# A decoder block on one core: two products of a Strassen-Winograd pair change places, the next pair's weight splits follow them, and the last combinations go between chunks of p4

## The chip, the core and the metric

The kernel runs on one core of one Trainium2 chip. Its time is the device time of one execution in microseconds; the times shown for the kernel before come from three runs. The profile is one further execution, recorded by the hardware profiler; its own time is given beside its span, because the two differ a little. The engines are named as the profile names them: PE (matmuls, with PEld for weight loads), DVE (vector), ACT (scalar), POOL (GpSimd) and SP (which here only issues transfers).

## What is computed

The reference is one decoder layer on 512 tokens of width 1024 in float32:

```python
h = rmsnorm(x, pre_mix_norm)
proj = h @ w_in          # q_r, k_r, v_r, g_r, q_s, k_s, v_s, gate_r, gate_s
ret = silu(g_r) * groupnorm(retention(q_r, k_r, v_r))
y_r = ret @ w_ret_out
y_s = swa_gqa_sinks(q_s, k_s, v_s, sinks) @ w_swa_out
merged = sigmoid(gate_r) * y_r + sigmoid(gate_s) * y_s
x = x + rmsnorm(merged @ w_out, post_mix_norm)
h = rmsnorm(x, pre_mlp_norm)
u = square(relu(h @ w_up))            # 1024 -> 4096
x = x + rmsnorm(u @ w_down, post_mlp_norm)   # 4096 -> 1024
```

## The kernel before, in words

**Precision by splitting.** Every large product is made of three matmuls in a reduced format: an operand is split into a high part and a low part (`split`, L119 to L122). ACT casts the high part (L121), DVE subtracts it from the source to get the low part (L122). `mm3` (L162 to L166) then multiplies high by high (L164), high by low (L165) and low by high (L166). In the profile a line of `split` or `mm3` stands for all of its callers, so groups are told apart by the names of the tiles: `whi` and `wlo` are split weights from the pool `stream`, `p` (in the code p24 and p22) are split weights from the pool `wx` or `px`.

**Gate and up projections in pairs.** The two gate projections (8 pairs of 256 columns: r and s in turn) and 13 of the 16 pairs of the up projection use a seven-product scheme for 2x2 blocks (Strassen-Winograd). For one pair, `wino_weights` (L203) prepares the left operands from two tiles: `raw`, which `wino_load` (L196) fills by two SP transfers (L199, L200: a11 and a12 in one, a22 in the other), and `rs`, the sums s1 and s3, which `wino_sums` (L189) fills by one SP transfer (L192) and one accumulating POOL transfer (L193). It splits a11 and a12 (p1: `whi`, `wlo`), then rs (p31: `whi`, `wlo`), adds a11 and a12 into rs (L208, L209), splits that into p24 (s2 and s4) and splits a22 into p22. `wino_pair` (L221) then issues the products in the order 11·11, 12·21, s2·t2, s4·22, s1·t1, s3·t3, 22·t4. Each `product` is four `mm3`, that is 12 matmuls, so a pair is 84 matmuls. Around them DVE and ACT combine the banks: L240 to L242 after the first three products, L246 and L249 after s1·t1 and s3·t3, L251 last.

**What limits how far ahead the weights are made.** `raw` has two buffers, `whi` and `wlo` four each, `rs` two in the gate stage and three in the up stage, p24 and p22 one each. So p24 of the next pair can be written only when s4·22 of this pair is done, and p22 only when 22·t4 is done. The transfer into a `raw` buffer waits until the pair that used the buffer has made its last split from it, which is p22's. In the profile p22's parts appear as `p<-raw` and p24's as `p<-rs`.

**Who sets the order.** Each engine executes its queue in order. The queues are laid out when the kernel is built, from the order of the source lines as priority and from when operands and buffers come free; so a line that stands earlier in the source goes first when both are ready, but the queues are not simply the source order. `tc.high_priority` moves a block ahead.

**Callers.** In the gate stage `gate` (L698) makes the weights of a pair, runs `wino_pair`, applies the sigmoid on ACT (L711) and for s multiplies into ys (L713). After the pairs r and s of each of the first three `bp` comes `ret_proj` (L717), which loads 1024 KB of w_ret_out into a `raw` buffer (L137), splits it into two `whi`/`wlo` pairs and makes two blocks of 24 matmuls (tile `yr`). In the up stage `up_pair` (L922) does the same for w_up with relu and square on ACT (L933, L934), into the tile `uc`.

**The end of the kernel.** The down projection is another seven-product scheme over 4 chunks `j` of the inner dimension, with two token blocks `tb`. p1, p2 and p5 come first, then p6, p3 and p7 interleaved (L1071 to L1079). L1082 to L1090 combine p6, p3 and p7 on DVE and call `finish` (L1018), which squares and sums on ACT (L1023), scales on DVE (L1027, L1028 or L1031, L1035, L1038), takes a power on POOL (L1034) and stores (L1041). Then p4 is made: chunks 0 and 1 (24 matmuls each), then chunks 2 and 3 for each token block in turn (24 matmuls each), with the last combination L1101 and `finish` after each block. For each chunk `left` (L954) splits the activations and `right` (L959) the summed weights `tch` in two halves; `left` has two buffers.

Of the kernel before, what the change touches and what calls it, by code (L numbers as in the profile page):

```python
# [20 lines left out]
KD = D_MODEL // P  # L21
# [70 lines left out]
def block_kernel(ctx, tc, x, pre_mix, w_in, w_gate, w_ret, w_swa, w_out, sinks, post_mix,  # L92
                 pre_mlp, w_up, w_down, post_mlp, decay, chunk, dist, out):
    nc = tc.nc
    x, out = x[0], out[0]
# [100 lines left out]
    def wino_load(w):  # L196

        raw = raw_tile([P, 3, 4, P])
        nc.sync.dma_start(raw[:, 0:2], w[:, 2:4])  # L199
        nc.sync.dma_start(raw[:, 2], w[:, 0])  # L200
        return raw

    def wino_weights(wx, rs, raw, px=None):  # L203

        a11, a12, a22 = raw[:, 0], raw[:, 1], raw[:, 2]
        p1 = parts(raw[:, :2], [P, 2, 4, P])
        p31 = parts(rs, [P, 2, 4, P])
        nc.vector.tensor_tensor(rs[:, 0], rs[:, 0], a11, op=ALU.add)  # L208
        nc.vector.tensor_tensor(rs[:, 1], rs[:, 0], a12, op=ALU.add)  # L209
        p24 = [(px or wx).tile([P, 2, 4, P], F32R, name=f"p24{i}") for i in range(2)]  # L210
        split(p24[0], p24[1], rs)
        p22 = [wx.tile([P, 4, P], F32R, name=f"p22{i}") for i in range(2)]
        split(p22[0], p22[1], a22)
        return {
            "11": tuple(a[:, 0] for a in p1), "12": tuple(a[:, 1] for a in p1),
            "22": tuple(p22),
            "s1": tuple(a[:, 0] for a in p31), "s3": tuple(a[:, 1] for a in p31),
            "s2": tuple(a[:, 0] for a in p24), "s4": tuple(a[:, 1] for a in p24),
        }

    def wino_pair(wx, a, b, out):  # L221

        p16 = bank([P, 2, 256], "wino")
        p57 = bank([P, 2, 256], "wino")
        p2 = bank([P, 256], "wino")
        p34 = bank([P, 2, 256], "wino")

        def product(ps, x, y):
            for k in range(4):
                mm3(  # L230
                    ps, tuple(o[:, k] for o in a[x]), tuple(o[:, k] for o in b[y]),
                    k == 0, k == 3,
                )

        pc = wx.tile([P, 256], F32, name="pc", bufs=2)
        q = wx.tile([P, 3, 256], F32, name="q")
        product(p16[:, 0], "11", "11")
        product(p2, "12", "21")
        product(p16[:, 1], "s2", "t2")
        nc.scalar.copy(pc, p16[:, 0])  # L240
        nc.vector.tensor_tensor(out[:, 0], p2, pc, op=ALU.add)
        nc.vector.tensor_tensor(q[:, 0], pc, p16[:, 1], op=ALU.subtract)  # L242
        product(p34[:, 0], "s4", "22")
        product(p57[:, 0], "s1", "t1")
        product(p57[:, 1], "s3", "t3")
        nc.vector.tensor_tensor(  # L246
            q[:, 1:3], p57, q[:, 0:1].to_broadcast([P, 2, 256]), op=ALU.add
        )
        nc.vector.tensor_tensor(out[:, 3], p57[:, 0], q[:, 2], op=ALU.add)  # L249
        product(p34[:, 1], "22", "t4")  # L250
        nc.vector.tensor_tensor(out[:, 1:3], p34, q[:, 1:3], op=ALU.add)  # L251


    hctx = ExitStack()
# [350 lines left out]
    for h in range(RET_HEADS):  # L605
# [20 lines left out]
        g = load_feature_pair(w_in, C_GR + h * RET_DV)  # L626
# [47 lines left out]
    wx = wino_pool(gctx)  # L674
# [20 lines left out]

    rsum = [gate_sums(0)]

    def gate(name, bp):  # L698
        i = bp + (KD // 2 if name == "s" else 0)
        if len(rsum) < len(gates):  # L700
            rsum.append(gate_sums(len(rsum)))
        a = wino_weights(wx, rsum[gates.index((name, bp))], wino_load(w_gate[i]))
        if name == "s":
            g = sgpool.tile([P, 4, 256], F32, name="sgs", bufs=1)
        else:
            g = sgpool.tile([P, 4, 256], F32, name="sgr", bufs=4)
        wino_pair(wx, a, hB, g)
        for b in range(2):
            fb = 2 * bp + b
            sg = g[:, 2 * b : 2 * b + 2].rearrange("p h c -> p (h c)")  # L710
            nc.scalar.activation(sg, sg, AF.Sigmoid, scale=(1.0, -1.0)[b])  # L711
            if name == "s":
                nc.vector.tensor_tensor(ys[fb], ys[fb], sg, op=ALU.mult)  # L713
            else:
                sig[fb] = sg

    def ret_proj(bp):  # L717

        wr = load_feature_pair(w_ret, bp * 256)
        for b in range(2):  # L720
# [7 lines left out]
            nc.vector.tensor_tensor(sig[fb], ps, sig[fb], op=ALU.mult)  # L728
            nc.vector.tensor_add(sig[fb], sig[fb], ys[fb])

    for bp in range(KD // 2):
        gate("r", bp)
        gate("s", bp)
        if bp in YR_AT:
            ret_proj(YR_AT[bp])
    gctx.close()
# [178 lines left out]
    def load_t(j):  # L915
        pool = dpool2 if j == 0 else dpool3
        tch[j] = pool.tile([P, 4, 512], F32, name=f"tch{j}")
        nc.sync.dma_start(tch[j], w_down[0, 0, j])

    usum = []  # L920

    def up_pair(fp):  # L922
        while len(usum) < 16 - NH and len(usum) < fp - NH + 3:
            f = len(usum) + NH
            pool, bufs = (dpool2, 1) if f % 3 == 2 else (rspool, 2)
            usum.append(wino_sums(pool, w_up[f], bufs))
        a = wino_weights(wx, usum[fp - NH], wino_load(w_up[fp]), px)
        j, i = fp // 4, fp % 4
        r = uc[j][:, :, i]
        wino_pair(wx, a, h2B, r)  # L930
        for b in range(2):
            rb = r[:, 2 * b : 2 * b + 2]
            nc.scalar.activation(rb, rb, AF.Relu, scale=(1.0, -1.0)[b])  # L933
            nc.scalar.activation(rb, rb, AF.Square)  # L934
        if i == 3:
            nc.vector.tensor_tensor(uc[j][:, 1], uc[j][:, 3], uc[j][:, 1], op=ALU.subtract)

    load_t(0)
    for fp in range(NH, 16):
        up_pair(fp)  # L940
    uctx.close()
    dpool3 = ctx.enter_context(tc.tile_pool(name="dpool3", bufs=1))
    for j in range(1, 4):
# [7 lines left out]
    def banks2(name):  # L951
        return [bank([P, 512], name) for _ in range(2)]

    def left(j, q):  # L954
        hi, lo = (ring.tile([P, 4, 256], F32R, name=f"left{i}") for i in range(2))
        split(hi, lo, uc[j][:, q])
        return hi, lo

    def right(src):  # L959
        return [parts(src[:, 2 * i : 2 * i + 2], [P, 2, 512]) for i in range(2)]  # L960
# [8 lines left out]
    def product2(ps, j, a, b):  # L969
        for h in range(2):  # L970
            for tb in range(2):
                product(ps, a, b, h, j == 0, j == 3, tb)
# [106 lines left out]
    step_p7(3)  # L1079


    for tb in range(2):  # L1082
        nc.vector.tensor_tensor(p15[tb], p6[tb], p15[tb], op=ALU.subtract)
        nc.vector.tensor_tensor(u3[tb], p6[tb], p1c[tb], op=ALU.subtract)
        nc.vector.tensor_tensor(p1c[tb], p3[tb], p15[tb], op=ALU.add)
        finish(tb, 1, p1c[tb])
        nc.vector.tensor_tensor(u3[tb], p7[tb], u3[tb], op=ALU.add)
        v = fin.tile([P, 512], F32, name="c", bufs=4)
        nc.vector.tensor_tensor(v, p7[tb], p15[tb], op=ALU.add)
        finish(2 + tb, 1, v)  # L1090


    p4 = banks2("p4")
    for j in range(2):
        product2(p4, j, left(j, 3), right(tch[j]))
    ab = [(left(j, 3), right(tch[j])) for j in (2, 3)]
    for tb in range(2):
        for j in (2, 3):
# [33 lines left out]
```

## Time and profile before

| what | value |
|---|---|
| median of 3 runs (lowest, highest) | 770.73 us (764.59, 771.12) |
| the profiled execution's own time | 767.67 us |
| its span, first to last instruction | 765.9 us |
| PE busy | 746.0 us, 4676 matmuls |
| DVE busy | 538.1 us |
| ACT busy | 392.5 us |
| gate stage with the retention projections between | about 255 to 390 us of the span |
| pairs of the up stage | about 462 to 600 us |
| down projection and end | about 600 to 766 us |

How to read it: the profiled execution took 767.67 us, of which 1.77 us lie outside the span. A busy PE is not PE at its peak, since the ends of matmuls are modelled; what can be read off is where PE waited and for whom. A row of the waits gives "engine line waited for: us in total, times, longest us". A row of a timeline gives the start, the duration, the engine, the line, and in brackets the idle time before it and who ended it. A row of the table by stretches gives for each engine the busy time and in parentheses the number of instructions, then the granted TensorE clock (1.00 is full), the share of the DMA engines and GB/s.

### The profile page before, as it was taken

What the parts mean: (1) busy time and instruction counts of PE and PEld (TensorE: products, weight loads), DVE (VectorE), ACT (ScalarE), POOL (GpSimd) and SP (SyncE); (2) the same over time, 40 slices, a digit from 0 to 9 for tenths busy, and PEclk for the clock granted to TensorE, in tenths of its full rate; (3) what the DMA queues carried; (4) which work ended last, traced back from release to release, by engine and by line L of the source; (5) the groups of instructions that cost most, each with busy time, mean ns of one, the idle gap of its engine ahead of it and who ended that gap; (6) DMA issues with size and microseconds to landing.
All of it is one profiled execution on the core that took longest, in us unless ns stands there. A gap on an engine that the chain in (4) does not pass through costs nothing.

```text
span 765.9 us, 11626 instructions
## 1 busy us (share of the span) xinstructions
PE 746.0 (97%) x4676; PEld 670.0 (87%) x4676; DVE 538.1 (70%) x823; ACT 392.5 (51%) x627; POOL 49.7 (6%) x65
## 2 busy tenths in 40 slices
PE   7999999999999999999999999999999999999986
PEld 6989889898888989899888999999989888888864
DVE  5473484564868966766754876867678688988795
ACT  6354463464454634343543764545466565655551
POOL 1100000000001000000001100000000010010000
PEclk9999999999999999999999999999999999999998
DMA  8151312302016566452572517765563899199511
GB/s 287 36 150 45 110 56 84 110 28 83 29 56 151 150 202 173 124 143 79 203 294 79 152 43 224 203 157 153 174 165 97 277 304 216 56 185 200 110 55 55
DMA packets 50007, 105.22 MB, mean 137 GB/s; under 512 B 2977, under 2 KB 30753, under 8 KB 46114
## 3 DMA queue, kind: packets, MB, share of 16 engines
q1 hardware_dynamic: 44914, 78.80, 30.6%
q0 software_dynamic: 5040, 25.69, 18.1%
q8 instruction: 36, 0.59, 0.3%
q14 instruction: 17, 0.14, 0.1%
HBM read 102.38 MB, written 2.10 MB: 136 GB/s over the span
## 4 chain that ended last, share of the span: by engine, by line
PE 72%; DMA 11%; DVE 9%; issue 4%; ACT 3%; POOL 0%; SPq 0%; POOLq 0%; DVEq 0%; ACTq 0%
DMA raw<-in_w_up 6%; PE pblk L166 5%; PE wino L166 5%; PE pblk L165 5%; PE pblk L164 5%; PE wino L164 5%; PE wino L165 5%; PE p L165 4%; PE p L166 4%; PE p L164 4%; DVE wlo L122 2%; PE ptok L166 2%; PE ptok L164 2%; PE ptok L165 2%; PE yr L165 2%
## 5 line engine op out<-in xcount | busy, mean ns | idle before, releaser
L122 DVE TENSOR_TENSOR wlo<-raw,whi 128x1024 fp32r<-128x1024 f32 x91 | 110.8, 1221 | 98.3 <-ACT whi L121 90.9
L121 ACT CAST whi<-raw 128x1024 fp32r<-128x1024 f32 x91 | 95.1, 1050 | 116.3 <-PE pblk L165 36.5
L165 PE MATMUL p<-wlo,left 128*128 128x512 f32 x224 | 87.5, 391 | 2.4 <-DVE wlo L122 2.3
L166 PE MATMUL p<-whi,left 128*128 128x512 f32 x224 | 87.5, 391 | 1.2 <-DVE left L122 1.0
L164 PE MATMUL p<-whi,left 128*128 128x512 f32 x224 | 87.1, 390 | 0.1
L166 PE MATMUL pblk<-hT,wlo 128*128 128x512 f32 x160 | 62.4, 390 | 0.5 <-DVE wlo L122 0.5
L164 PE MATMUL pblk<-hT,whi 128*128 128x512 f32 x160 | 62.6, 391 | 0.0
L165 PE MATMUL pblk<-hT,whi 128*128 128x512 f32 x160 | 62.3, 390 | 0.0
L165 PEld LDWEIGHTS p<-wlo,left 128*128 128x128 f32 x224 | 42.0, 188 | 12.1 <-DVE wlo L122 3.2
L166 PEld LDWEIGHTS p<-whi,left 128*128 128x128 f32 x224 | 42.0, 188 | 11.3 <-DVE left L122 2.8
L164 PEld LDWEIGHTS p<-whi,left 128*128 128x128 f32 x224 | 42.0, 188 | 9.4 <-ACT left L121 0.9
L164 PE MATMUL ptok<-whi,hT 128*128 128x256 f32 x160 | 46.5, 290 | 0.6 <-ACT hT L121 0.6
L166 PE MATMUL ptok<-whi,hT 128*128 128x256 f32 x160 | 45.9, 287 | 1.1 <-DVE hT L122 1.1
L165 PE MATMUL ptok<-wlo,hT 128*128 128x256 f32 x160 | 45.8, 286 | 0.0
L121 ACT CAST left<-uc 128x1024 fp32r<-128x1024 f32 x28 | 29.3, 1050 | 28.1 <-PE p L165 28.1
L122 DVE TENSOR_TENSOR wlo<-tch,whi 128x1024 fp32r<-128x1024 f32 x32 | 38.6, 1219 | 5.2 <-ACT whi L121 5.2
L121 ACT CAST whi<-tch 128x1024 fp32r<-128x1024 f32 x32 | 33.4, 1047 | 12.9 <-PE p L166 8.1
L122 DVE TENSOR_TENSOR left<-uc,left 128x1024 fp32r<-128x1024 f32 x28 | 34.1, 1220 | 7.9 <-ACT left L121 7.9
L166 PEld LDWEIGHTS pblk<-hT,wlo 128*128 128x128 f32 x160 | 30.0, 188 | 7.2 <-DVE wlo L122 0.9
L164 PEld LDWEIGHTS pblk<-hT,whi 128*128 128x128 f32 x160 | 30.1, 188 | 5.8
L165 PEld LDWEIGHTS pblk<-hT,whi 128*128 128x128 f32 x160 | 30.0, 188 | 5.8
L166 PE MATMUL wino<-h2s,p 128*128 128x256 f32 x104 | 30.2, 291 | 4.4 <-DVE p L122 4.1
(291 smaller groups left out, 2196.1 us busy)
## 6 DMA issues: line engine op xcount, KB each, us to landing
tch<-in_w_down POOLq DMA_DIRECT2D x10, 1024.0 KB, 10.1
raw<-in_w_in SPq DMA_DIRECT2D x9, 1024.0 KB, 5.5
raw<-in_w_down SPq DMA_DIRECT2D x7, 1024.0 KB, 8.5
rs<-in_w_up SPq DMA_DIRECT2D x13, 512.0 KB, 4.6
rs<-in_w_up POOLq DMA_DIRECT2D x13, 512.0 KB, 5.6
raw<-in_w_up SPq DMA_DIRECT2D x13, 512.0 KB, 5.3
raw<-in_w_in SPq DMA_DIRECT2D x12, 512.0 KB, 4.2
raw<-in_w_gate SPq DMA_DIRECT2D x8, 512.0 KB, 5.8
```

The costliest lines, as they stand in the source:

```text
L121: nc.scalar.copy(hi, src)
L122: nc.vector.tensor_tensor(lo, src, f(hi), op=ALU.subtract)
L164: nc.tensor.matmul(ps, ah, bh, start=first, stop=False)
L165: nc.tensor.matmul(ps, ah, bl, start=False, stop=False)
L166: nc.tensor.matmul(ps, al, bh, start=False, stop=last)
```

## The change

Three edits. In `wino_pair` the product 22·t4 moves from the last place to the fifth, straight behind s4·22, and a callback `then` is called there: it makes the weights of the next pair, so that their loads and splits stand in the source behind the last use of s2, s4 and a22 and ahead of s1·t1, s3·t3 and what combines them. The gate and up stages are rewritten around that: the weights of the first pair are made before the loop, and each pair returns the next pair's. In the gate stage the weights of the next r pair so come ahead of `ret_proj`, which stood ahead of them. At the end, the combinations of p6, p3 and p7 become a function `combine(tb)`, called behind chunk 0 of p4 for token block 0 and behind chunk 1 for block 1. No operation is added or removed.

```diff
-    def wino_pair(wx, a, b, out):
+    def wino_pair(wx, a, b, out, then=None):
...
         product(p34[:, 0], "s4", "22")
+        product(p34[:, 1], "22", "t4")
+        nxt = then() if then else None
         product(p57[:, 0], "s1", "t1")
         product(p57[:, 1], "s3", "t3")
         nc.vector.tensor_tensor(
             q[:, 1:3], p57, q[:, 0:1].to_broadcast([P, 2, 256]), op=ALU.add
         )
         nc.vector.tensor_tensor(out[:, 3], p57[:, 0], q[:, 2], op=ALU.add)
-        product(p34[:, 1], "22", "t4")
         nc.vector.tensor_tensor(out[:, 1:3], p34, q[:, 1:3], op=ALU.add)
+        return nxt
...
-    def gate(name, bp):
-        i = bp + (KD // 2 if name == "s" else 0)
+    def gate_weights(n):
+        name, bp = gates[n]
         if len(rsum) < len(gates):
             rsum.append(gate_sums(len(rsum)))
-        a = wino_weights(wx, rsum[gates.index((name, bp))], wino_load(w_gate[i]))
+        return wino_weights(wx, rsum[n], wino_load(w_gate[bp + (KD // 2 if name == "s" else 0)]))
+
+    def gate(n, a):
+        name, bp = gates[n]
...
-        wino_pair(wx, a, hB, g)
+        a = wino_pair(wx, a, hB, g, (lambda: gate_weights(n + 1)) if n < len(gates) - 1 else None)
...
+    a = gate_weights(0)
     for bp in range(KD // 2):
-        gate("r", bp)
-        gate("s", bp)
+        a = gate(2 * bp, a)
+        a = gate(2 * bp + 1, a)
         if bp in YR_AT:
             ret_proj(YR_AT[bp])
...
-    def up_pair(fp):
+    def up_weights(fp):
         while len(usum) < 16 - NH and len(usum) < fp - NH + 3:
...
-        a = wino_weights(wx, usum[fp - NH], wino_load(w_up[fp]), px)
+        return wino_weights(wx, usum[fp - NH], wino_load(w_up[fp]), px)
+
+    def up_pair(fp, a):
...
-        wino_pair(wx, a, h2B, r)
+        a = wino_pair(wx, a, h2B, r, (lambda: up_weights(fp + 1)) if fp < 15 else None)
...
+    a = up_weights(NH)
     for fp in range(NH, 16):
-        up_pair(fp)
+        a = up_pair(fp, a)
...
-    for tb in range(2):
+
+    p4 = banks2("p4")
+    def combine(tb):
         nc.vector.tensor_tensor(p15[tb], p6[tb], p15[tb], op=ALU.subtract)
...
         finish(2 + tb, 1, v)
 
-
-    p4 = banks2("p4")
     for j in range(2):
         product2(p4, j, left(j, 3), right(tch[j]))
+        combine(j)
```

More of the change, by code (lines that the diff above doesn't have):

```diff
@@ L715, in gate @@
                 sig[fb] = sg
+        return a
     def ret_proj(bp):
@@ L936, in up_pair @@
             nc.vector.tensor_tensor(uc[j][:, 1], uc[j][:, 3], uc[j][:, 1], op=ALU.subtract)
+        return a
     load_t(0)
+    a = up_weights(NH)
     for fp in range(NH, 16):
-        up_pair(fp)
+        a = up_pair(fp, a)
     uctx.close()
```

## The prediction, on record before the change was run

> **What bounds the kernel now.** I read the page first, then the waits of PE, then the busy time by stretches.
>
> ```profile
> span 765.9 us, 11626 instructions
> PE 746.0 (97%) x4676; PEld 670.0 (87%) x4676; DVE 538.1 (70%) x823; ACT 392.5 (51%) x627; POOL 49.7 (6%) x65
> ```
>
> ```profile
> PE wino L166 <- DVE p L122: 4.1, 4, 1.3
> PE p L165 <- DVE wlo L122: 2.3, 1, 2.3
> ```
>
> ```profile
> 250.00:460.00 210.00, 209.94 (x1377) 192.48 (x1377) 147.08 (x197) 102.51 (x167) 12.43 (x16) 1.00 0.50 150
> 503.00:570.00 67.00, 62.73 (x511) 61.36 (x510) 46.14 (x66) 34.57 (x54) 5.24 (x6) 1.00 0.63 167
> ```
>
> PE bounds the kernel, so a change of order can win only where PE waits. The gate stage has 0.06 us of such time in 210. The up stage has 67.00 - 62.73 = 4.27 us between 503 and 570; the waits give 4.1 of it to p, the split weights p24 and p22. The end has one wait of 2.3 us. These two waits, 6.4 us or 0.8% of the time, are all that the change can take away.
>
> What paces the up stage is seen in the chain of waits, one turn of it:
>
> ```profile
> 545.07 0.61 DVE p L122
> ...
> 545.69 5.51 DMA raw<-in_w_up
> ...
> 551.23 1.06 ACT whi L121
> ...
> 552.45 1.00 issue
> 553.45 0.68 DVE q L246
> ...
> 554.21 0.98 issue
> 555.18 0.42 DVE uc L249
> 555.60 0.60 DVE uc L251
> 556.20 0.61 DVE p L122
> ...
> 556.83 5.68 DMA raw<-in_w_up
> ```
>
> The turn is a loop. The low part of p22 (545.07) is the last reader of a raw buffer, so the next load starts behind it. The load takes 5.51 us, then ACT casts (1.06). The two stretches of "issue" are DVE's subtractions for a11/a12 and for the sums (1.00 and 0.98). Queued behind the first of them, though they need nothing of this load, are L246, L249 and L251 of an earlier pair; behind these stands p22's low part, which releases the next load. The turn is 556.83 - 545.69 = 11.14 us.
>
> ```profile
> 488.77 0.33 SPq L199 DMA_DIRECT2D raw<-in_w_up  x1
> 568.13 0.33 SPq L199 DMA_DIRECT2D raw<-in_w_up  x1
> ```
>
> ```profile
> 482.80 0.28 PE L164 MATMUL wino<-h2c,whi 128*128 128x256 f32 x1
> 482.92 0.28 PE L165 MATMUL wino<-h2c,whi 128*128 128x256 f32 x1
> ...
> 556.85 0.39 PE L166 MATMUL wino<-h2s,p 128*128 128x256 f32 x1 [0.79 <-DVE p L122]
> ```
>
> Seven turns take 568.13 - 488.77 = 79.36 us, 11.34 each. PE starts a matmul every 0.12 us, so a pair of 84 needs 10.08 and a product of 12 needs 1.44. Each turn loses 1.26, in seven turns 8.8 us; PE lost only 4.27, so about 4.5 us were a lead of the weights over PE that was used up first. The wait at 556.85 ends when p22's low part does (556.20 + 0.61): that split sets the end of the stage.
>
> **Edit 1: 22·t4 fifth, and the next weights behind it.** Nothing is added or removed. PE's 84 matmuls stay 10.08 us. p22 comes free two products (2.88 us) earlier and is needed 2.88 us earlier, so its own window does not change. What changes is who stands ahead of it. L246, L249 and L251 of a pair can run only after its last product now, 2.88 us behind the moment at which p22 of the next pair comes free, and their source lines stand behind those splits. I therefore expect p22's low part ahead of them in DVE's queue. Out of the turn go L246 (0.68), the sums' subtraction (0.98), L249 (0.42) and L251 (0.60), together 2.68: 11.14 - 2.68 = 8.46 us. What could come in instead are the combinations of the first three products and p24's low part:
>
> ```profile
> 547.58 0.42 DVE L241 TENSOR_TENSOR uc<-wino,pc 128x256 f32<-128x256 f32 x1 [0.59 <-ACT pc L240]
> 547.92 0.41 DVE L242 TENSOR_TENSOR q<-pc,wino 128x256 f32<-128x256 f32 x1
> 548.53 1.22 DVE L122 TENSOR_TENSOR p<-rs,p 128x1024 fp32r<-128x1024 f32 x1 [0.19 <-ACT p L121]
> ```
>
> With all three, 0.42 + 0.41 + 1.22 = 2.05, the turn is 10.51. At the low end PE (10.08) is the bound and the stage waits for nothing; at the high end 12 turns lose 12 x 0.43 = 5.2 us, of which the lead of 4.5 hides all but 0.7. So the 4.1 us go, or 3.4 of them; I take **-4.1**, because in the turn shown all three (547.58 to 549.75) are done before the load has landed (551.2), which puts them outside the turn. L246 to L251 become 2.88 us later; what hides this is that their banks are wanted only by the pair after the next, ten microseconds on. Without that cover it would be 0.68 + 0.42 + 0.60 = 1.7 us a pair. The transfers of the sums (L192, L193) keep their place in SP's queue ahead of the raw loads; they wait for p24, which is not moved.
>
> **Edit 1 in the gate stage.** There is nothing to win here (0.06 us), only to lose. The load of w_ret_out (1024 KB) now comes behind the weights of the next r pair, so it gets the raw buffer of the s pair instead of the r pair's, and cannot start before p22 of the s pair is split.
>
> ```profile
> 265.44 0.28 PE L164 MATMUL wino<-hT,whi 128*128 128x256 f32 x1
> ...
> 275.52 0.40 PE L164 MATMUL yr<-retT,whi 128*128 128x512 f32 x1
> ```
>
> ```profile
> 255.92 0.38 SPq L137 DMA_DIRECT2D raw<-in_w_ret_out  x1
> ```
>
> ```profile
> 267.23 0.68 DVE L122 TENSOR_TENSOR p<-raw,p 128x512 fp32r<-128x512 f32 x1
> ```
>
> ```profile
> tch<-in_w_down POOLq DMA_DIRECT2D x10, 1024.0 KB, 10.1
> ...
> raw<-in_w_ret_out SPq DMA_DIRECT2D x4, 1024.0 KB, 5.2
> ```
>
> ```profile
> L122 DVE TENSOR_TENSOR wlo<-raw,whi 128x1024 fp32r<-128x1024 f32 x91 | 110.8, 1221 | 98.3 <-ACT whi L121 90.9
> L121 ACT CAST whi<-raw 128x1024 fp32r<-128x1024 f32 x91 | 95.1, 1050 | 116.3 <-PE pblk L165 36.5
> ```
>
> The first s pair starts at 265.44 and its p22 is done at 267.91; the retention product starts at 275.52. From 267.91 the load (5.2), the cast (1.05) and the subtraction (1.22) end at 275.4, in time by 0.1. With p22 freed 2.88 us sooner the margin is 3.0. I take **0**; the other end is the slowest row of that size, 10.1 us from 267.91, which is 280.3: 4.8 us late at each of three places, +14.3.
>
> **Edit 2: the combinations between chunks of p4.** The wait of 2.3 us is here:
>
> ```profile
> 742.33 0.39 PE L164 MATMUL p<-whi,left 128*128 128x512 f32 x1
> 744.98 0.50 PE L165 MATMUL p<-wlo,left 128*128 128x512 f32 x1 [2.26 <-DVE wlo L122]
> ```
>
> ```profile
> 736.27 0.68 DVE L1087 TENSOR_TENSOR u<-p,u 128x512 f32<-128x512 f32 x1
> ...
> 743.10 0.68 DVE L1028 TENSOR_TENSOR c<-c,g_out 128x512 f32<-128x512 f32 x1
> 743.70 1.22 DVE L122 TENSOR_TENSOR wlo<-tch,whi 128x1024 fp32r<-128x1024 f32 x1
> ...
> 750.51 1.22 DVE L122 TENSOR_TENSOR wlo<-tch,whi 128x1024 fp32r<-128x1024 f32 x1
> ```
>
> ```profile
> 724.50:751.70 27.20, 26.27 (x33) 1.00 0.10 39
> ```
>
> PE waits for the second half of chunk 1 (743.70), which stands behind the combinations of both token blocks. With block 1's moved behind chunk 1, that wait goes. But DVE is busy for 26.27 of the 27.20 us up to the last split (750.51 + 1.22), and PE still has 30 matmuls behind that split. All of DVE's work ahead of the last split stays ahead of it if block 1's combination runs before chunks 2 and 3, as in the source; then PE, early by 2.3 us, waits for the last split instead. Only what slips behind that split is won. The ends are 0 and -2.3; nothing of the same work can end later than now except by a wait inside it, so no loss is added. I take **-0.5**, near the DVE-bound end.
>
> **Sum.** 767.67 - 4.1 + 0 - 0.5 = 763.1 us against the profiled execution's own time. The median shown is 3.1 above that time. Each turn of the loop holds one transfer, and 0.25 us more in each of 12 gives 3 us; if that is the cause, it goes as well, so I leave 763.1 for the median too.
>
> **The rivals.** *The whole wait at the end goes too*: the last steps of block 1 (L1028, L1035, L1038) wait for a square on ACT and a power on POOL and could slip behind the last splits. Against it stands the full DVE. 763.1 - 1.8 = 761.3 us.
>
> *The queue stays as it is (slower).* The change doesn't do what it says if p22's low part is still laid behind L246, L249 and L251. For it speaks that DVE's queue does not follow the source now: weights two pairs ahead of L246 stand before it. Against it, that p22 is free first. The turn then stays 11.34, and since 22·t4 comes two products sooner, PE needs p22 2.88 us earlier and the lead is smaller by that: 767.67 + 2.9 - 0.5 = 770.1 us. It decides at p22's place: ahead of L246 or behind.
>
> *The retention weights come late (slower).* If SP's queue holds the load of w_ret_out behind transfers that wait, or it takes as long as the row of 10.1, PE waits up to 4.8 us at three places: 763.1 + 14.3 = 777.4 us. It decides once the split is later than 275.52, that is a load issued more than 7.5 us ahead of the product or not. For it speaks that a start of 255.92, twenty microseconds ahead, is given up; against it the margin of 3.0.
>
> In no wait of this trace does the clock fall: the stretch with the longest, 2.26 us, ran at 1.00.
>
> ```profile
> 742.00:746.00 4.00, 1.74 (x8) 1.12 (x7) 4.00 (x7) 1.42 (x2) 0.00 (x0) 1.00 0.35 131
> ```
>
> The Trainium skill, "TensorE: Matmul & The Clock Gate", section "HAM oscillation — how this bites in real kernels", says that idle gaps beyond about 3.4 us halve the clock until PE has been busy for such a window again. By that rule the three waits of 4.8 us would cost an estimated 1.7 us more each, and the last rival would be 782.5 us. No wait here is long enough to test it.
>
> **How the numbers follow.** The forecast has 0.60, the whole end 0.12, the unchanged queue 0.17, the late retention weights 0.11. A measurement of this kernel can tell about 1%, 7.7 us. Against the shown median the forecast is 1.0% faster, against the profiled execution 0.6%, so half of it and of the first rival count as faster by over 1%: 0.36, taken as 0.35. Slower by over 1% is the last rival, 0.10; the rest, 0.55, is within. The range leaves the last rival out: from 761.3 less the 3.1 by which the lowest run shown lies under the profiled one, 758.2, up to the highest shown, 771.1.
>
> **What would show it right or wrong.** Right: in the up stage p22's low part stands before L246 in DVE's rows, the SP issues of L199 come every 10.1 us, and PE's wait for p is under 0.5 us in total; no wait at yr; at the end PE's wait moves from chunk 1 to the last split of chunk 3. Wrong: turns of 11 us or more, waits at yr L164 to L166, or a new wait of DVE or ACT that reaches PE in the gate stage.

## The result and the profile after

The changed kernel takes 759.77 us (median of 6 runs, 758.68 to 760.97), the kernel before in the same comparison 767.66 (6 runs, 764.59 to 771.12). The ratio is 0.990, with a 95% interval of 0.986 to 0.993. The forecast was 763.1 in a range of 758.2 to 771.1. The profiled execution after has a time of its own of 760.97 us and a span of 759.1, so it lies 6.7 us (6.8 in the span) under the profiled execution before.

The lines of the changed kernel are numbered a little further down: L241 and L242 of before are L242 and L243, L246, L249 and L251 are L249, L252 and L253, and L1028, L1035, L1038 are L1040, L1047, L1050.

The head of the page of the kernel after:

```profile
span 759.1 us, 11633 instructions
PE 744.1 (98%) x4676; PEld 670.9 (88%) x4676; DVE 539.5 (71%) x823; ACT 393.3 (52%) x627; POOL 50.2 (7%) x65
```

The waits of PE after (total, times, longest):

```profile
PE p L165 <- DVE wlo L122: 2.1, 1, 2.1
...
PE wino L166 <- DVE p L122: 0.6, 1, 0.6
...
PE yr L166 <- DVE wlo L122: 0.2, 1, 0.2
```

And the busy time by stretches, the same two as before:

```profile
250.00:460.00 210.00, 209.74 (x1378) 192.25 (x1377) 147.99 (x198) 102.39 (x167) 12.42 (x16) 1.00 0.50 150
...
503.00:570.00 67.00, 67.00 (x561) 67.00 (x560) 55.70 (x78) 40.34 (x62) 5.24 (x6) 1.00 0.71 182
```

Between 503 and 570 PE no longer waits at all (67.00 of 67.00, before 62.73). The gate stage has 0.26 us of idle time instead of 0.06, and the wait at the end is still there.

One turn of DVE in the up stage after, in order of time:

```profile
522.97 1.22 DVE L122 TENSOR_TENSOR wlo<-raw,whi 128x1024 fp32r<-128x1024 f32 x1
524.10 1.22 DVE L122 TENSOR_TENSOR p<-rs,p 128x1024 fp32r<-128x1024 f32 x1
525.24 0.68 DVE L122 TENSOR_TENSOR p<-raw,p 128x512 fp32r<-128x512 f32 x1
525.84 0.68 DVE L249 TENSOR_TENSOR q<-wino,q 128x512 f32<-128x512 f32 x1
526.55 0.42 DVE L252 TENSOR_TENSOR uc<-wino,q 128x256 f32<-128x256 f32 x1
526.90 0.68 DVE L253 TENSOR_TENSOR uc<-wino,q 128x512 f32<-128x512 f32 x1
527.49 1.21 DVE L122 TENSOR_TENSOR wlo<-rs,whi 128x1024 fp32r<-128x1024 f32 x1
```

The low part of p22 (525.24), which releases the next load, stands ahead of L249, L252, L253 and of the sums' subtraction, as forecast. The loads follow each other accordingly:

```profile
497.37 0.33 SPq L199 DMA_DIRECT2D raw<-in_w_up  x1
...
566.58 0.33 SPq L199 DMA_DIRECT2D raw<-in_w_up  x1
```

Seven turns take 69.21 us, 9.89 each instead of 11.34; PE needs 10.08 for a pair. So the loads are no longer what PE waits for.

**Where the time came from.** Three starts of PE's matmuls cut the run into stages: the first product of the up stage, the first of the down projection and the last matmul of all. Before:

```profile
462.64 0.28 PE L164 MATMUL wino<-h2c,whi 128*128 128x256 f32 x1
...
600.06 0.40 PE L164 MATMUL p<-whi,left 128*128 128x512 f32 x1
...
758.30 0.39 PE L166 MATMUL p<-whi,left 128*128 128x512 f32 x1
```

After:

```profile
462.59 0.28 PE L164 MATMUL wino<-h2c,whi 128*128 128x256 f32 x1
...
594.57 0.40 PE L164 MATMUL p<-whi,left 128*128 128x512 f32 x1
...
751.47 0.39 PE L166 MATMUL p<-whi,left 128*128 128x512 f32 x1
```

Up stage 137.42 to 131.98 us: -5.44. Down projection 158.24 to 156.90: -1.34. Everything ahead of the up stage: -0.05. What follows the last matmul: 7.6 in both. The sum is -6.83, the difference of the spans.

The -1.34 has two parts. From the first to the 73rd matmul of the down projection (at 618.38 and 610.92) it is 18.32 us before and 16.35 after: -1.97. The rest, 139.92 and 140.55, is 0.63 longer after; behind its wait at the end the granted clock was 0.50 for 3.41 us, which is shown further down.

### The profile page after: what moved, and what is told of

The parts are those of the page before. It is cut to its first block, busy times and chain, and to the rows that moved or that the text cites. A ratio compares the mean times of both kernels' runs of the same rounds, so it can differ in the third digit from the quotient of the medians.

```text
span 759.1 us, 11633 instructions
## 1 busy us (share of the span) xinstructions
PE 744.1 (98%) x4676; PEld 670.9 (88%) x4676; DVE 539.5 (71%) x823; ACT 393.3 (52%) x627; POOL 50.2 (7%) x65
## 4 chain that ended last, share of the span: by engine, by line
PE 82%; DVE 8%; DMA 5%; issue 2%; ACT 2%; POOL 0%; POOLq 0%; DVEq 0%; SPq 0%; ACTq 0%
PE wino L166 8%; PE wino L165 8%; PE wino L164 8%; PE pblk L166 5%; PE pblk L165 5%; PE pblk L164 5%; PE p L165 4%; PE p L166 4%; PE p L164 4%; DVE wlo L122 3%; PE ptok L166 2%; PE ptok L164 2%; PE ptok L165 2%; PE yr L166 2%; PE yr L164 2%
## 5 line engine op out<-in xcount | busy, mean ns | idle before, releaser
L165 PEld LDWEIGHTS p<-wlo,left 128*128 128x128 f32 x224 | 42.5, 190 | 11.9 <-DVE wlo L122 3.1
L121 ACT CAST whi<-rs 128x1024 fp32r<-128x1024 f32 x21 | 22.0, 1050 | 31.2 <-PE yr L165 11.5
```

Source lines behind the costliest of these rows:

```text
L121: nc.scalar.copy(hi, src)
L165: nc.tensor.matmul(ps, ah, bl, start=False, stop=False)
```

## The experiments

Each kernel was timed in five rounds beside the kernel before; a ratio is to the kernel before, with its 95% interval. "Up" is the time from the first product of the up stage to the first of the down projection, "down" from there to the last matmul, both in the profiled execution (before: 137.42 and 158.24). One execution differs from the next: the up stage with the old order of products takes 134.98 to 138.10 us in the three profiles of the table that have it; with the new order and no extra work in it, 131.04 to 133.56.

| kernel | median us | ratio | up | down |
|---|---|---|---|---|
| changed kernel, again (e5_again) | 760.50 | 0.990 (0.987 to 0.994) | 131.77 | 155.85 |
| edit 1 alone (e1_pairs) | 762.07 | 0.990 (0.988 to 0.992) | 131.04 | 156.68 |
| edit 2 alone (e2_comb) | 767.90 | 0.999 (0.998 to 1.000) | 134.98 | 159.13 |
| 22 by t4 fifth alone (e3_order) | 760.87 | 0.990 (0.988 to 0.991) | 131.57 | 156.49 |
| weights early, 22 by t4 last (e4_call) | 769.19 | 1.000 (0.999 to 1.002) | 137.80 | 157.97 |
| edit 1 in the gate stage alone (e8_gate) | 770.14 | 1.001 (0.998 to 1.003) | 138.10 | 160.12 |
| changed, block 1's combinations last (e6_last) | 760.40 | 0.990 (0.987 to 0.994) | 131.18 | 156.24 |
| changed, multiplications on POOL (e7_pool) | 762.47 | 0.992 (0.990 to 0.995) | 133.56 | 158.00 |
| changed, more DVE work inside the loop (e9_in) | 766.71 | 0.996 (0.995 to 0.998) | 135.19 | 157.80 |
| changed, the same work outside it (e10_out) | 763.91 | 0.994 (0.992 to 0.996) | 134.30 | 155.87 |
| changed, steps of two tiles deferred (e11_defer) | 756.99 | 0.985 (0.983 to 0.988) | 131.71 | 153.29 |
| before, 22 by t4 fifth, steps deferred (e12_least) | 757.59 | 0.987 (0.983 to 0.991) | 131.26 | 153.95 |

The theory was that one thing is worth almost everything: the place of p22's low part in DVE's queue, since the next load waits for it. The rivals were that the early writing of the weights matters, or that edit 2 carries part of it.

### The two edits apart

e1_pairs is the changed kernel with edit 2 taken back:

```diff
-    p4 = banks2("p4")
-    def combine(tb):
+    for tb in range(2):
...
-        combine(j)
```

> Edit 1 alone, the combinations where they were before. My theory: edit 1 carries the whole gain. First to last matmul of the up stage's pairs 131.9 us (137.30 before, 131.86 after), no wait of PE for left between 600 and 614 (1.0 us before), and at the end the old wait of 2.3 us for the second half of chunk 1. Time 760 us, ratio to before 0.990, within 1 us of the kernel with both edits. Rival: edit 2 carries some 2 us of the 8; then 762 us, ratio 0.993.

e2_comb is the kernel before with edit 2:

```diff
-    for tb in range(2):
+    p4 = banks2("p4")
+    def combine(tb):
...
         product2(p4, j, left(j, 3), right(tch[j]))
+        combine(j)
```

> Edit 2 alone, the pairs as before. My theory: nothing is won, since DVE's work ahead of the last split is the same; PE's wait of 2.3 us moves from chunk 1 to chunk 2 or 3, and the granted clock may fall to 0.50 for 3.4 us behind it as in the profile after, which costs 1.7 more. Up stage 137.3 us as before, time 767.5 to 769.5 us, ratio 1.000 to 1.002. Rival: the wait goes with the edit, 765.4 us, ratio 0.997.

Measured: edit 1 alone has the ratio of both edits, 0.990; edit 2 alone has 0.999, at most 0.2% under 1. In e2_comb PE's waits for p stay (2.7 us) and the wait of 2.2 us at the end is there too, in another place. The gain is edit 1's. The median of e1_pairs, 762.07, is the rival's figure, but its ratio is not: the interval ends at 0.992, the rival had 0.993. From the other side the interval of e2_comb leaves edit 2 at most 1.8 us. So the rival of 2 us is out, by little.

### The two halves of edit 1

e3_order changes one line of the kernel before:

```diff
         product(p34[:, 0], "s4", "22")
+        product(p34[:, 1], "22", "t4")
         product(p57[:, 0], "s1", "t1")
...
-        product(p34[:, 1], "22", "t4")
```

> Only 22 by t4 moved to the fifth place; the weights of a pair are still made after the pair before it, and the combinations stay where they were. In DVE's queue of this kernel p22's low part stands ahead of L247, L250 and L251 all the same. My theory: the place of that split in the queue is what counts, so the whole gain is here: up stage 132 us, loads of L199 every 9.9 us, time 760 to 761 us, ratio 0.991. Rival: the weights must also be written inside the pair; then the turn stays at 11.3 us and PE needs p22 2.88 us sooner, 767.7 to 770.6 us, ratio 1.000 to 1.004.

e4_call is the changed kernel with edit 2 taken back and 22·t4 last among the products again, so that the callback which writes the next weights stands behind all seven products and still ahead of the last combinations:

```diff
         product(p34[:, 0], "s4", "22")
+        product(p57[:, 0], "s1", "t1")
+        product(p57[:, 1], "s3", "t3")
         product(p34[:, 1], "22", "t4")
         nxt = then() if then else None
-        product(p57[:, 0], "s1", "t1")
-        product(p57[:, 1], "s3", "t3")
```

> The weights of the next pair written inside the pair, ahead of its last combinations, but 22 by t4 last as before; the combinations at the end as before. In DVE's queue p22's low part then stands behind L249, L252 and the sums' subtraction, and ahead of L253 alone. My theory: the turn gets at most the 0.60 us of L253 shorter, 10.7 us and still over PE's 10.08, so most of the wait stays: up stage 134 to 137 us, time 765 to 767.7 us, ratio 0.997 to 1.000. Rival: the early writing is what counts, 760 us, ratio 0.990.

Measured: the one moved line has the whole gain (0.990), the callback without it has none (1.000). In e3_order, where the weights are still made after the pair, DVE's rows have the new order all the same:

```profile
526.73 0.69 DVE L122 TENSOR_TENSOR p<-raw,p 128x512 fp32r<-128x512 f32 x1
527.33 0.68 DVE L247 TENSOR_TENSOR q<-wino,q 128x512 f32<-128x512 f32 x1
```

(L247 here is L246 of before.) The source order of the splits and the combinations is as it was, and so is the amount of DVE's work; p22 is free earlier, and that is enough to bring its split forward in the queue that was built. In e4_call the split stands behind L249, L252 and the sums' subtraction, as expected; its turns are 10.48 us (eight of them between the issues of L199 at 497.09 and 580.90), shorter than the 11.34 of before. Its up stage is no shorter in the profile, though, because PE first waits 3.7 us, and it also loses time in the gate stage. The profiled execution is the slowest of the twelve (772.98 us, the median is 769.19), so the size of these waits need not hold for the others; what caused the wait of 3.7 stays open. The waits of PE in e4_call:

```profile
PE wino L164 <- ACT p L121: 3.7, 1, 3.7
...
PE yr L164 <- ACT whi L121: 1.8, 2, 1.2
PE yr L166 <- DVE wlo L122: 1.2, 2, 0.7
```

These 3.0 us at yr are the prediction's last rival, the late retention weights: here w_ret_out is loaded behind a p22 that comes free only at the end of a pair, and its first load is issued at 268.22 instead of 264.75.

### Edit 1 in the gate stage alone

e8_gate uses the new order and the callback for the gate pairs, and the old order for the up pairs:

```diff
-        product(p34[:, 1], "22", "t4")
+        if not late:
+            product(p34[:, 1], "22", "t4")
...
-        a = wino_pair(wx, a, h2B, r, (lambda: up_weights(fp + 1)) if fp < 15 else None)
+        wino_pair(wx, a, h2B, r, late=True)
```

> Edit 1 in the gate stage alone; the up stage and the end as before. My theory: nothing is won or lost in the gate stage (0.06 us of idle before, 0.26 after), so 767 to 769 us, ratio 1.000; loads of w_ret_out are issued some 9 us later than before and take up to 9 us. Rival: the loads come late in most executions and cost 1 to 3 us: ratio 1.002 to 1.004.

Measured: 1.001 (0.998 to 1.003), nothing that can be told from no change. In its profile PE waits 0.5 us at yr, and the up stage is as before. So the gain of edit 1 comes from the up stage and what follows it.

### What the end waits for

e5_again is the changed kernel itself.

> The changed kernel once more, as the yardstick for the next three. Question: does the half clock behind the last wait (0.50 for 3.4 us in the profile after and behind a wait of 2.16 us with edit 2 alone, but not behind waits of 2.25 us with edit 1 alone or with 22 by t4 moved alone) come back? Theory: it is a matter of how the wait falls into a time grid, so it comes in some executions and costs 1.7 us when it does; time 759 to 762 us, ratio 0.990. Rival: it belongs to the place of the combinations and comes each time.

e6_last:

```diff
-        combine(j)
+        if j == 0:
+            combine(0)
     ab = [(left(j, 3), right(tch[j])) for j in (2, 3)]
+    combine(1)
```

> The changed kernel with the combinations of block 1 written behind the splits of chunks 2 and 3 instead of ahead of them. In DVE's queue, L1103 and L1040 of block 1 (0.6 us each at their spacing) then stand behind splits of chunk 3. My theory: DVE's work ahead of the last split bounds the end, so the wait of 2.1 us falls by about 1.2, and the half clock is less likely: 757 to 759.5 us, 0.997 of the changed kernel. Rival: the wait is about something else than the amount; no difference, or slower by what block 1's results are later (up to 1.3 us).

e7_pool (only the calls inside the combinations pass POOL, `nc.gpsimd`):

```diff
-            nc.vector.tensor_tensor(src, src, g_out[:, c], op=ALU.mult)
+            eng.tensor_tensor(src, src, g_out[:, c], op=ALU.mult)
...
-        finish(tb, 1, p1c[tb])
+        finish(tb, 1, p1c[tb], nc.gpsimd)
...
-        finish(2 + tb, 1, v)
+        finish(2 + tb, 1, v, nc.gpsimd)
```

> The changed kernel with the four multiplications by g_out (L1040, L1047 inside the combinations) on POOL instead of DVE. They are 4 of 0.68 us, 2.4 us at their spacing, all ahead of the last split. My theory: DVE's amount ahead of the last split bounds the end, so the wait of 2.1 us goes: 756.5 to 759 us, 0.996 of the changed kernel. Rival: POOL is slower for such work (its 128x256 copy takes 0.73 us, so 1.4 us for 128x512) and what DVE does next with these results waits in front of the splits; then the wait stays or grows by up to 1.5 us: 760 to 763 us.

Measured: the half clock of the first profile did not come back in e5_again, whose down projection is 1.05 us shorter (155.85 against 156.90); more on that below. e6_last is the same as the changed kernel (760.40 and 760.50). Its wait of 2.1 us at the end is shorter, 1.23, and now stands at the left of the last chunk; but another wait of 0.84 appeared at 694, so its profile neither bears the theory out nor refutes it. e7_pool is a miss: its median is 2 us above the changed kernel's, not below, though the intervals of the two ratios overlap, and 1.8 us of its profile lie in the up stage (133.56 against 131.77), which the edit does not touch. POOL's rows, and DVE's of the same moment:

```profile
731.49 2.06 POOL L1040 TENSOR_TENSOR c<-c,g_out 128x512 f32<-128x512 f32 x1 [6.89 <-ACT junk L1035]
733.51 2.28 POOL L1047 TENSOR_TENSOR p1c<-p1c,g_out 128x512 f32<-128x512 f32 x1
```

```profile
732.37 2.26 DVE L122 TENSOR_TENSOR wlo<-tch,whi 128x1024 fp32r<-128x1024 f32 x1
```

A multiplication takes 2.06 and 2.28 us on POOL (0.68 on DVE), and the DVE split beside them takes 2.26 instead of 1.22. Much of what was taken off DVE came back as slower DVE work, so this run says nothing about DVE's amount.

e11_defer answers that. It takes the last steps for the first two output tiles out of the combinations and writes them behind the splits of chunks 2 and 3:

```diff
         nc.vector.tensor_tensor(p1c[tb], p3[tb], p15[tb], op=ALU.add)
-        finish(tb, 1, p1c[tb])
...
     ab = [(left(j, 3), right(tch[j])) for j in (2, 3)]
+    for tb in range(2):
+        finish(tb, 1, p1c[tb])
```

> The changed kernel with the last steps for the first two output tiles (square, L1043, L1047, L1050 for blocks 0 and 1, 2.4 us of DVE each) written behind the splits of chunks 2 and 3. In DVE's queue block 0's stand ahead of the last two splits and block 1's behind the last split. My theory: DVE's amount ahead of the last split bounds the end, so the wait of 2.1 us goes: last matmul minus first matmul of the down projection 154 us (155.85 and 156.90 in two runs of the changed kernel), time 758 us, 0.997 of the changed kernel. Rival: what is moved comes back behind the last matmul, where the last tiles' steps wait for DVE: no difference.

Measured: 756.99 us, ratio 0.985 (0.983 to 0.988). That is below the kernel before by far, and below the changed kernel's 0.990, whose interval it just touches; no wait of PE for wlo is left in the down projection, and it takes 153.29 us. Nothing comes back at the end: behind the last matmul there are 7.6 us as before. Block 1's steps now run behind the last split:

```profile
739.68 1.22 DVE L122 TENSOR_TENSOR wlo<-tch,whi 128x1024 fp32r<-128x1024 f32 x1
...
740.93 0.68 DVE L1047 TENSOR_TENSOR p1c<-p1c,g_out 128x512 f32<-128x512 f32 x1
```

From the first split of p7's last weights (716.78) to the end of the last split (740.90) it is 24.1 us; in the changed kernel 26.7 (717.15 to 743.81), in the kernel before 27.2 (724.52 to 751.73).

e12_least combines that with the one moved line, on the kernel before, without callback and without edit 2.

> The kernel before with two small edits only: 22 by t4 moved to the fifth place, and the last steps for the first two output tiles written behind the splits of chunks 2 and 3; the weights are made after the pair and the combinations stand together ahead of chunk 0, as before. My theory: the product order carries all of edit 1, and the amount of DVE work ahead of the last split, not the place of the combinations, sets the end; so this is as fast as the changed kernel with the deferred steps: 757 us, ratio 0.985, no wait over 1 us in the down projection. Rival: the combinations between the chunks are needed as well; then the wait for the second half of chunk 1 stays at 2.2 us less what was moved (1.2 to 2.4), 758 to 760.5 us, ratio 0.987 to 0.990.

Measured: 757.59 us, ratio 0.987 (0.983 to 0.991); the longest wait in the down projection is 0.62 us. So neither the callback nor the combinations between the chunks are needed; one moved line and the deferred steps are as fast as e11_defer within the intervals. The median is some 3 us under the changed kernel's, with intervals that overlap.

### Is it the loop or DVE's amount of work

e9_in and e10_out add the same work to the up stage of the changed kernel (the same values are computed again), once between landing and release of the load, once behind it:

```diff
         split(p22[0], p22[1], a22)
+        for _ in range(2 if px else 0):
+            nc.vector.tensor_tensor(p22[1], a22, f(p22[0]), op=ALU.subtract)
```

```diff
         p31 = parts(rs, [P, 2, 4, P])
+        for _ in range(2 if px else 0):
+            nc.vector.tensor_tensor(p31[1][:, 1], rs[:, 1], f(p31[0])[:, 1], op=ALU.subtract)
```

> The changed kernel with p22's low part computed three times in the up stage (the same values, 128x512 each), so two times 0.60 us more on DVE between the load's landing and the next load's start. My theory: this loop paces the stage. In the changed kernel its own length is load 4.8, cast 1.06, low parts 1.0, 1.14 and 0.60 and in some turns L242 and L243 0.7, that is 8.6 to 9.3; with 1.2 to 1.9 more it is 9.8 to 11.2 against PE's 10.08, so PE loses up to 1.1 in a turn less a lead of a few us: 761.5 to 767 us, turns over 10.2 us. Rival: DVE is idle for a sixth of this stage, so 1.2 us a turn are hidden: 760.5 us.

> The changed kernel with the same extra work on DVE (two times 128x512 a pair in the up stage, half of the low part of s1 and s3 recomputed), but behind p22's split in DVE's queue, where the load runs. My theory: outside the loop it costs nothing, 760.5 us, turns 9.9 to 10.1 us. Rival: DVE as such is the limit; then as slow as the kernel with the extra work inside the loop.

Measured: 766.71 us inside, as expected; 763.91 outside, where I expected no cost. The stretch from 503 to 570 in e9_in:

```profile
503.00:570.00 67.00, 66.04 (x547) 65.55 (x546) 59.36 (x86) 38.90 (x60) 5.24 (x6) 1.00 0.70 175
```

And in e10_out:

```profile
503.00:570.00 67.00, 64.68 (x535) 64.07 (x534) 58.50 (x84) 37.13 (x56) 5.24 (x6) 1.00 0.65 172
```

The turns are 10.4 us in both (seven of them: 72.81 and 73.05 us). DVE is busy for 58 to 59 us of 67 (55.70 without the extra work). Half of the theory falls here: work behind the release is not free once DVE has 8 to 9 us in 67 to spare. A likely reason is that it pushes the next pair's first split back in a queue that is this full; no run here shows that by itself. These two runs also do not tell the load loop from DVE's amount of work: 0.996 and 0.994 have intervals that overlap. That the place in the queue counts rests on e3_order, where the amount of work is the same as before.

## Why the prediction was right, and where it was not

**What bounds the kernel: right, but the price of a wait was too small.** "These two waits, 6.4 us or 0.8% of the time, are all that the change can take away" was too low: the spans differ by 6.8 with the end wait still there. One wait of the kernel before shows why:

```profile
544.09 0.28 PE L165 MATMUL wino<-h2s,p 128*128 128x256 f32 x1
545.72 0.39 PE L166 MATMUL wino<-h2s,p 128*128 128x256 f32 x1 [1.35 <-DVE p L122]
545.94 0.28 PE L164 MATMUL wino<-h2s,p 128*128 128x256 f32 x1
```

Two steps of 0.12 took 1.85 us, so 1.61 were lost, not 1.35. The idle time is counted from the modelled end of the matmul before (0.28 behind its start), though the next would have started 0.12 behind it; and the one after the wait follows at 0.22. So idle time understates what a wait costs. Over the whole stage, 13 pairs of 10.08 us need 131.04 and took 137.42: 6.4 us were lost, against 4.27 of idle time. By the same count the lead of the weights was 8.8 - 6.4 = 2.4 us and not 4.5.

**Edit 1 in the up stage: the mechanism was right, the term mis-sized.** -4.1 was forecast, -5.44 measured. The turn was put between 8.46 and 10.51 and is 9.89, under PE's 10.08, and the stage is left with 131.98 - 131.04 = 0.9 us of loss. What I had left outside the turn did come into it (the high end): p24's low part in the turn shown above, and in others L242 and L243 as well, ahead of p22's low part at 516.19:

```profile
514.39 0.42 DVE L242 TENSOR_TENSOR uc<-wino,pc 128x256 f32<-128x256 f32 x1
514.72 0.41 DVE L243 TENSOR_TENSOR q<-pc,wino 128x256 f32<-128x256 f32 x1
```

The loads became shorter at the same time: their median is 4.8 us after and was 5.3 before. Why they did is not shown, so that half a microsecond a turn was not earned by the argument. PE's total wait for p was to be under 0.5 us; it is 0.6, in one wait at 486.6 in the third pair, none behind it.

**A term that was missing: the start of the down projection.** The kernel before waited twice for left there:

```profile
601.08 0.50 PE L166 MATMUL p<-whi,left 128*128 128x512 f32 x1 [0.39 <-DVE left L122]
...
613.26 0.50 PE L166 MATMUL p<-whi,left 128*128 128x512 f32 x1 [0.63 <-DVE left L122]
```

The list of PE's waits before has them (1.0 us in two), but the sum left them out. Counted by the starts of matmuls, they are the 1.97 us at the start of the down projection. The first wait hangs on DVE's order: the split of left stands behind the first split of w_down's first load, and that one waited for its cast:

```profile
598.00 1.23 DVE L122 TENSOR_TENSOR wlo<-raw,whi 128x1024 fp32r<-128x1024 f32 x1 [2.08 <-ACT whi L121]
...
599.81 2.35 DVE L122 TENSOR_TENSOR left<-uc,left 128x1024 fp32r<-128x1024 f32 x2
```

After, left is split by 593.92, ahead of the stage. The second wait hangs on the load of chunk 1's tch, whose split stands ahead of the next left:

```profile
600.25 9.43 DMA tch<-in_w_down
```

After, the same load is issued just as late (594.76, 0.2 us behind the start of the stage) but takes 4.7 us. What differs is what runs beside it. The first two loads of w_down go through the same raw buffers as the pairs; the second is issued at the end of these rows, 4 us ahead of the stage before and 11 us after:

```profile
587.52 8.76 SPq L979 DMA_DIRECT2D raw<-in_w_down  x2
```

```profile
575.38 8.23 SPq L991 DMA_DIRECT2D raw<-in_w_down  x2
```

Before, this second load takes 9.8 us and so runs on beside the load of tch; after, it takes 4.8 and is long done. That loads slow each other down is the likely link, but no run tests it alone. That the term belongs to the new order in the up stage is shown: the first 72 matmuls take 17.82 to 18.56 us in the four profiles with the old order (before, e2_comb, e4_call, e8_gate) and 16.35 in nine of the ten with the new one (17.26 in e9_in, with its extra work). I had followed the freed buffer into the next pair and not past the end of the stage.

**Edit 1 in the gate stage: right, on a margin that was used up.** Forecast 0; measured 0.2 us of idle time, at one place of three, and a ratio of 1.001 for the stage alone. The chain of waits after:

```profile
264.04 0.70 DVE p L122
264.75 9.10 DMA raw<-in_w_ret_out
273.87 1.06 ACT whi L121
274.96 1.24 DVE wlo L122
```

The load is issued when it was expected, but takes 9.10 us and not 5.2 (6.2 to 9.1 for the four), so the margin of 3.0 became a wait of 0.2. For the load the other end (10.1) was the better price, but the loss put on it was too high: it counted the 10.1 from 267.91 and so left out the 2.88 us that p22 is free earlier; with them the 4.8 at each place are 1.9. With the buffer freed at the end of the pair the profile of e4_call has 3.0 us of waits at yr.

**Edit 2: right that it wins next to nothing, with the place wrong.** -0.5 was forecast; alone it is 0.999 (0.998 to 1.000), and in the profile after, the down projection behind its start is 0.63 us longer, with the half clock in it. The wait moved, not to the last split of chunk 3 but to the first of chunk 2, which stands behind block 1's last steps in DVE's queue. PE and DVE around it, after:

```profile
737.45 0.68 DVE L1040 TENSOR_TENSOR c<-c,g_out 128x512 f32<-128x512 f32 x1
738.05 3.49 DVE L122 TENSOR_TENSOR wlo<-tch,whi 128x1024 fp32r<-128x1024 f32 x3
...
739.32 0.50 PE L165 MATMUL p<-wlo,left 128*128 128x512 f32 x1 [2.12 <-DVE wlo L122]
```

The reason given, DVE's work ahead of the last split, is what e11_defer and e12_least bear out: with less of it the wait goes, with the combinations between the chunks or without.

**The queue that stays as it is** is out for this change (it has the split ahead of L249), and so is **the whole wait at the end goes too**.

**The number.** In the profiled executions 4.6 us were forecast and 6.7 measured: 1.3 more in the up stage, 2.0 at the start of the down projection that no term had, 1.1 less at the end. The median, 759.77, is 3.3 us under the forecast and still in the range, because the range's low end (758.2) was taken from the rival of the whole end wait less the spread of the runs. That rival is out, so the low end was right by luck.

**The clock.** "In no wait of this trace does the clock fall" is wrong. The kernel before ran at half clock behind its first waits, 0.56 and 1.06 us between 9.7 and 11.9:

```profile
11.00:12.00 1.00, 0.14 (x1) 0.15 (x2) 1.00 (x3) 0.77 (x2) 0.00 (x0) 1.00 1.03 387
...
14.00:15.00 1.00, 1.00 (x7) 1.00 (x6) 1.00 (x2) 1.00 (x3) 0.00 (x0) 0.50 1.19 308
```

So "No wait here is long enough to test it" does not hold either: behind waits of about 1 us this trace already has a stretch at half clock, and the changed kernel has one behind a wait of 2.1.

**The median's excess** of 3.1 us over the profiled execution was put down to jitter of the loads. That was mostly the draw of three runs: in the 66 runs of the kernel before that stand beside these experiments the median is 769.1, 1.4 above. The twelve runs of the changed kernel spread from 758.2 to 762.1. Whether the loop widened the spread stays open.

## What to carry to other kernels

When loads pace a stage, follow the buffer that they go into: its last reader's place in the engine's queue sets the next load, and freeing it earlier can move that reader forward without touching its own source line. Follow it past the end of the stage as well, since the next stage's first loads wait for the same buffers and what they run beside changes with them. Where an engine is full up to the last operation that the bound engine needs, reordering in front of that operation only moves the wait; work has to go behind it.

## What the runs showed that was not expected

**A wait of 2.1 us can halve the clock.** The granted clock was 0.50 for 3.41 us behind the last wait of the changed kernel, and not behind the longer one of the kernel before. The clock's changes lie on a grid of 3.41 us in every run. Two cells of that grid around the wait, after:

```profile
736.35:739.76 3.41, 1.29 (x6) 0.77 (x5) 3.41 (x5) 3.39 (x5) 0.00 (x0) 1.00 0.29 109
739.76:743.17 3.41, 3.41 (x10) 2.64 (x9) 3.41 (x4) 0.17 (x1) 0.00 (x0) 0.50 0.00 0
```

Before:

```profile
740.10:743.51 3.41, 2.62 (x11) 1.82 (x11) 2.97 (x7) 3.21 (x4) 0.93 (x1) 1.00 0.06 21
743.51:746.92 3.41, 1.94 (x8) 1.61 (x9) 3.41 (x4) 0.11 (x1) 0.00 (x0) 1.00 0.36 133
```

After, the wait lies in one cell, which leaves PE busy for 38% of it, and the next cell runs at half clock, 10 matmuls instead of 16 or 17. Before, a wait of 2.26 straddles two cells (77% and 57%), and nothing happens. Around the end of the down projection, cells with PE busy for 0.43 and less were followed by half clock in every profile, and none of 0.51 and more was. In between it is mixed: 0.47 fell in e7_pool, 0.47 in e4_call and 0.48 in e12_least did not. At the start of the kernel the line lies elsewhere: there cells of 0.49 to 0.56 fell in eight profiles (0.52 before, behind the waits of 0.56 and 1.06) and one of 0.57 in e7_pool did not. So a cell in which PE is busy for less than about half is at risk, where a wait falls in the grid matters as much as its length, and PE's busy share alone does not give the edge. At the end it is worth about 1 us: 156.90 against 155.85 for the down projection in the two profiles of the changed kernel.

The Trainium skill, "TensorE: Matmul & The Clock Gate", section "What's actually happening", says that the clock falls to half after an idle window of about 3.4 us and that the window runs freely. The traces agree on the window and the half clock; they differ on what counts as idle: a window with PE busy for 38% of it was enough.

**POOL is no relief for DVE here.** The rows of e7_pool above have 2.06 and 2.28 us for a 128x512 multiplication on POOL and 2.26 for the DVE split beside them, which takes 1.22 elsewhere. The Trainium skill, "GPSIMD Engine Reference", section "1. Specifications", says that POOL shares its SBUF interfaces with VectorE, with contention where a VectorE instruction has two SBUF inputs; the split reads tch and whi, and the numbers agree. The same page's section "4.1 Engine selection" puts POOL at about twice VectorE's time for two inputs; here it is three times, 2.06 against 0.68.
